# A hybrid encoder layer: block products of the second MLP matrix in turns with quarters of the first, two-tile splits, and a plain last group

## The chip, the cores and the metric

The kernel runs on one core of a Trainium2 chip. The metric is device time in microseconds (us) of one execution. Three executions of the kernel before took 756.33, 757.04 and 757.73 us. A separate execution was profiled; its rows are what is read below. PE is the matrix engine, DVE the vector engine, ACT the scalar engine, POOL the general engine (it also issues transfers that add to their target), SP the queue that issues most plain transfers; PEld is PE's weight load.

## The reference

One encoder layer on 512 tokens of width 1024: a mixer (long convolutions beside dilated attention) and a squared-ReLU MLP, each between RMS norms. The change lies in the MLP and where the mixer hands over to it:

```python
x = x + gt1 * rmsnorm(y, g_post_mix[l])
h = rmsnorm(x, g_pre_mlp[l]) * (1.0 + sc2) + sh2
f = jnp.square(jax.nn.relu(h @ w_mlp1[l])) @ w_mlp2[l]     # 1024 -> 4096 -> 1024
x = x + gt2 * rmsnorm(f, g_post_mlp[l])
```

Everything is float32. PE works on a rounded type (float32r), so each operand is split into a rounded high part and the rest (hi and lo), and a product is three matmuls: hi hi, hi lo, lo hi (`mm3`, L606).

## The kernel before

**How order is set.** The layer is written as a list of operations. `Plan.order` (L291) then chooses, by estimated durations and priorities, one order for each engine, which the engines follow strictly. `plan.bias` and `plan.local` raise priorities; `plan.group` keeps the matmuls of one group at one priority; `_cost` (L529) holds the durations. An operation recorded on `vp` may go to DVE or POOL. Buffers come from named tags with a fixed count (`NB`): `w` 9, `wx` 12, `vx` 12, `cv` 22, `H` 9.

**First MLP product.** `hidden(cc, banks)` (L1383) makes 512 of the 4096 hidden features for all tokens: it loads 8 tiles of `w_mlp1` (256 KB each, on SP, into `raw`), splits each (`whi` by a cast on ACT, `wlo` by a subtraction on DVE or POOL), runs 8 x 4 x 3 = 96 matmuls of 512 columns into four PSUM banks (named `pm`), and squares the relu of the banks into four tiles `r`. There are eight such blocks.

**Second MLP product.** The 4096 features are taken in four groups of two blocks (`sb`). Each group is a product of a 2 x 2 block matrix (token halves by feature blocks) with a 2 x 2 block matrix of weights, done with 7 block products instead of 8. Each block product (`product`, named `pf`) has 4 x 2 x 3 = 24 matmuls into two banks. Some need sums of hidden blocks (`dif`, by `vp`) or of weight blocks. The latter are made by a transfer: `load` puts a weight block into `braw` on SP, and `more` adds another block to it on POOL's queue (`accum_op`). So `braw` of sum "s" serves products 4, 2, 1 and 6, each time after another addition; every user splits it anew into `whi` and `wlo`. The hidden half (128 x 256) is split too (`split_a`, into `ha`, ACT and DVE). Results are added over groups into seven pairs of `acc` tiles (two of them in the buffers of `mask` and `rope`). In the last group each product is added on arrival to the final blocks it belongs to, and a token tile is normalised (`early_half`, `late_half`), gated, added to x and stored once its two halves are there.

**What comes when.** Two blocks of `hidden` are made, then a third, then the 7 products of a group in a row in the order 4, 2, 1, 3, 6, 5, 7, then two more blocks, and so on, with falling priority (`begin`, L1448):

```python
next_hidden()
for sb in range(NS):
    next_hidden()
    next_hidden()
    ...
    product(4, diff(0, A21, A22), load("s", 0, 0))
    product(2, same(A22), more("s", 1, 0))
    product(1, diff(0, A11, D0), more("s", 1, 1))
    ...
```

Of the kernel before, what the change touches and what calls it, by code (L numbers as in the profile page):

```python
# [11 lines left out]
F32 = mybir.dt.float32  # L12
# [210 lines left out]
class Op:  # L223
    __slots__ = ("eng", "call", "dur", "lat", "preds", "succs", "bufs", "new", "n", "rt", "start", "prio", "idx", "move", "urgent", "table", "port", "alt", "group")


class Plan:
# [4 lines left out]
    def __init__(self, nc):  # L232
        self.nc, self.ops, self.tags, self.cnt = nc, [], {}, 0
        self.bias = self.local = 0.0
        self.group = 0
        self.pools = {}
# [17 lines left out]
    def record(self, eng, call, writes, reads, dur, lat=0.0, after=()):  # L254
# [3 lines left out]
        op.port, op.alt, op.group = eng == "gp", None, self.group  # L258
# [32 lines left out]
    def order(self):  # L291
# [58 lines left out]
        while len(done) < len(ops):  # L350
# [44 lines left out]
            if op.move is not None:  # L395

                dma = max(dma, end + 0.65) + op.move
                end = dma + 1.05
# [54 lines left out]
class _Engine:  # L453
# [35 lines left out]
    def __getattr__(self, meth):  # L489
        plan, eng = self.plan, self.eng  # L490

        def rec(*args, after=(), urgent=0.0, **kw):
# [15 lines left out]
            dur, lat = _cost(home, meth, args, kw, writes, reads)  # L508

# [13 lines left out]
            if meth == "dma_start":  # L523
                op.move, op.lat = lat, 0.0
            return op
# [30 lines left out]
def tile_hymba_layer(ctx, tc, t, out):  # L556
# [3 lines left out]
    FILTERS, INPUT, SOON, ROUND, LEAD = 200.0, 1000.0, 9000.0, 3000.0, 30.0  # L560
# [13 lines left out]
    for n in ("basis", "wx"):  # L574
        stage(n, "left")
    for n in ("xp", "hT", "att", "mp"):
        stage(n, "right", side="right")
    NB = {"H": 9, "vx": 12, "qk": 8, "cv": 22, "w": 9, "raw": 4, "ra": 3, "G": 3,
          "x": 8, "xa": 6, "h": 16, "m": 16, "wx": 12}
    HOME = {"x": "xp", "xa": "xp", "h": "hT", "m": "mp", "wx": "wx"}  # L580
# [4 lines left out]
    def R(tag, s="r"):  # L585
        return S(tag, s, F32R)
# [586 lines left out]


# [19 lines left out]
    def group_split(src, gcol, tag):  # L1194
        spl = []
        for i in range(4):
            hi, lo = R(tag, "mh"), R(tag, "ml")
# [35 lines left out]
    NPT = 8  # L1233
# [70 lines left out]
    ma = group_split(att, 108, "cv")  # L1304
# [3 lines left out]
    for tt in range(4):  # L1308
        for hf in range(2):
# [4 lines left out]
    h2T = [(R("m", "h2h"), R("m", "h2l"))  # L1314
           for _ in range(8)]
# [51 lines left out]
    wtags[:] = ["w", "wx"]  # L1367
# [4 lines left out]
    acc, ATAG = {}, ["H"] * 9 + ["G"] + ["cv"] * 2  # L1372
# [10 lines left out]
    def hidden(cc, banks):  # L1383

        ws = [wload(w_1[k * P:(k + 1) * P, cc * 512:cc * 512 + 512]) for k in range(8)]
        for th in range(2) if cc == 0 else (None,):
            ts = slice(0, 512) if th is None else slice(th * 256, th * 256 + 256)
            for k in range(8):
                for i in range(4):
                    s = slice(i * P, (i + 1) * P)  # L1390
                    mm3(banks[i][:, ts], ws[k][0][:, s], ws[k][1][:, s], h2T[k][0][:, ts], h2T[k][1][:, ts], k == 0, k == 7)
        res = []
        for i in range(4):
            r = S("vx", "r")
            act.activation(r, banks[i], AF.Relu)
            vp.tensor_tensor(out=r, in0=r, in1=r, op=ALU.mult)
            res.append(r)
        return res
# [22 lines left out]
    def late_half(tt, a, hf, q, other):  # L1421
# [5 lines left out]
        for i, o in ((1 - hf, other), (hf, g)):  # L1427
# [10 lines left out]
    TO = {1: ((7, 1), (6, 1)), 2: ((2, 1), (6, -1)), 3: ((6, 1), (5, 1)), 4: ((2, 1), (7, 1)), 5: ((7, -1), (5, 1)),  # L1438
          6: ((6, 1),), 7: ((7, 1),)}
    NS, KT = 4, 4  # L1440
    HALF = (slice(0, 256), slice(256, 512))
    NCC = 2 * NS

    hid, piece = {}, [0]

    def begin():  # L1448
        plan.local = LEAD * (NCC + NS - piece[0])
        piece[0] += 1  # L1450
        return piece[0] % 2

    def next_hidden():
        cc = len(hid)
        if cc < NCC:
            hid[cc] = hidden(cc, PS4(begin(), "pm"))
            step(late2)

    next_hidden()
    for sb in range(NS):  # L1460
        next_hidden()
        next_hidden()
        aa, ab = hid[2 * sb], hid[2 * sb + 1]
        last = sb == NS - 1
        tags = ("ps", "pi") if begin() else ("pj", "pj")
        pair = lambda n: [PS("pf", tags[n]) for _ in range(2)]
        wsrc = lambda r, k, c: w_2[sb * 1024 + r * 512 + k * P:sb * 1024 + r * 512 + (k + 1) * P, c * 512:c * 512 + 512]

        pairs = [0]

        def fresh():
            pairs[0] += 1
            plan.group += 1
            return pair((pairs[0] + 1) % 2)

        def add(eng, o, a, b, sign=1):
            eng.tensor_tensor(out=o, in0=a, in1=b, op=ALU.add if sign > 0 else ALU.subtract)

        def product(n, parts, raws):
            banks = fresh()  # L1480
            if last and n == 7:
                ws = [(split_w(raws(k)), parts(k)) for k in range(KT)]
                for i in range(2):
                    for k, ((wh, wl), a) in enumerate(ws):
                        mm3(banks[i], a[:, i * P:(i + 1) * P], a[:, 256 + i * P:256 + (i + 1) * P], wh, wl, k == 0, k == KT - 1)
                    arrive(n, i, banks[i])
                return
            for k in range(KT):
                wh, wl = split_w(raws(k))
                a = parts(k)  # L1490
                for i in range(2):
                    mm3(banks[i], a[:, i * P:(i + 1) * P], a[:, 256 + i * P:256 + (i + 1) * P], wh, wl, k == 0, k == KT - 1)
            for i in range(2):
                arrive(n, i, banks[i])

        def arrive(n, i, bank):
            if not last:
                put(n, i, bank)
                return
            for m, sign in TO[n]:  # L1500
                add(dve, acc[m, i], acc[m, i], bank, sign)

            if n == 2:
# [95 lines left out]
```

## Time and profile before

| what | us |
|---|---|
| median of three runs | 757.04 |
| the profiled execution | 759.21 |
| its span | 757.3 |
| PE busy in the span | 708.6 |
| DVE busy | 573.2 |
| ACT busy | 375.7 |
| POOL busy | 162.6 |
| first block product starts | 452.55 |
| last matmul starts | 746.26 |

The span runs from the first to the last instruction. A busy engine is one that executes; matmuls are pipelined and their ends are modelled, so PE's pace is better read from the number of matmuls that start in a stretch. A wait is idle time of an engine, put down to whatever ended it last. All operations are issued through one helper, line L514, so rows are told apart by the tile names, not by lines.

### The profile page before, as it was taken

To read this page: it belongs to the slowest core of one execution; us is meant where nothing else is said; L and a number is where in the kernel's file an instruction comes from. 1 tells how busy PE (TensorE), PEld (TensorE's weight loads), DVE (VectorE), ACT (ScalarE), POOL (GpSimd) and SP (SyncE) were. 2 spreads that over 40 slices of the span, in tenths; PEclk is the share of its full clock that TensorE was granted. 3 is DMA by queue.
4 is the path that set the end of the run, shared out by engine and by line. 5 is a ranking of instruction groups with operands and counts; after the bars stand their busy time and mean duration, and the time that the engine had idled before them with its cause. 6 is when DMAs were issued, how large, how long until landed. Compare 5 with 4: busy or idle time off the path is not lost. (4 is left out here: it accounts for less than half of the span.)

```text
span 757.3 us, 10569 instructions
## 1 busy us (share of the span) xinstructions
PE 708.6 (94%) x3552; PEld 564.6 (75%) x3552; DVE 573.2 (76%) x1113; ACT 375.7 (50%) x765; POOL 162.6 (21%) x169
## 2 busy tenths in 40 slices
PE   5999999999999999999989998999999999999693
PEld 2667878988897867778879876788777887778472
DVE  5497974989698679997978844656378555898897
ACT  5545442234224478886764524754354434544543
POOL 0120400113032134330120022100242004232440
PEclk9999999999999999999999999999999999999998
DMA  9995244433615363352216547533675337654643
GB/s 287 363 393 183 84 151 155 124 99 115 210 53 167 111 209 99 98 168 71 70 58 199 169 88 147 133 126 126 112 167 128 109 111 132 166 134 92 131 113 124
DMA packets 62518, 109.30 MB, mean 144 GB/s; under 512 B 6621, under 2 KB 15069, under 8 KB 62208
## 3 DMA queue, kind: packets, MB, share of 16 engines
q1 hardware_dynamic: 52096, 87.39, 35.5%
q0 software_dynamic: 10224, 21.18, 15.2%
q8 instruction: 28, 0.46, 0.3%
q14 instruction: 26, 0.21, 0.1%
q10 hardware_dynamic: 144, 0.06, 0.0%
HBM read 104.14 MB, written 4.46 MB: 143 GB/s over the span
## 5 line engine op out<-in xcount | busy, mean ns | idle before, releaser
L514 PE MATMUL pf<-whi,ha 128*128 128x512 f32 x448 | 135.2, 398 | 18.5 <-ACT whi L514 10.5
L514 DVE TENSOR_TENSOR wlo<-braw,whi 128x512 fp32r<-128x512 f32 x112 | 78.8, 725 | 55.4 <-ACT whi L514 49.3
L514 PEld LDWEIGHTS pf<-whi,ha 128*128 128x128 f32 x448 | 83.5, 190 | 44.1 <-ACT whi L514 16.2
L514 ACT CAST whi<-braw 128x512 fp32r<-128x512 f32 x112 | 67.6, 619 | 82.8 <-DMA braw<-in_w_mlp_dram 66.6
L514 ACT CAST whi<-raw 128x512 fp32r<-128x512 f32 x128 | 77.1, 619 | 58.3 <-PE pj L514 27.9
L514 POOL DMA_DIRECT2D braw<-in_w_mlp_dram x64 | 55.9, 929 | 212.5 <-DVE wlo L514 116.4
L514 PE MATMUL pm<-h2h,whi 128*128 128x512 f32 (+1 forms) x288 | 91.8, 374 | 2.9 <-DVE y L514 2.1
L514 DVE TENSOR_TENSOR wlo<-raw,whi 128x512 fp32r<-128x512 f32 x111 | 75.9, 698 | 22.4 <-ACT whi L514 10.7
L514 PE MATMUL pm<-h2l,whi 128*128 128x512 f32 (+1 forms) x288 | 92.1, 374 | 0.0
L514 PE MATMUL pm<-h2h,wlo 128*128 128x512 f32 (+1 forms) x288 | 90.9, 372 | 0.0
L514 PE MATMUL pf<-wlo,ha 128*128 128x512 f32 x224 | 79.0, 396 | 1.6 <-DVE wlo L514 1.6
L514 PEld LDWEIGHTS pm<-h2h,whi 128*128 128x128 f32 x288 | 53.3, 190 | 13.5 <-DVE y L514 2.3
L514 PEld LDWEIGHTS pm<-h2l,whi 128*128 128x128 f32 x288 | 53.4, 190 | 10.8 <-issue 0.5
L514 PEld LDWEIGHTS pm<-h2h,wlo 128*128 128x128 f32 x288 | 53.2, 190 | 10.0
L514 PEld LDWEIGHTS pf<-wlo,ha 128*128 128x128 f32 x224 | 42.2, 189 | 13.5 <-DVE wlo L514 4.9
L514 DVE SCALAR_TENSOR_TENSOR acc<-raw,vec,acc 128x512 f32<-128x512 f32 x56 | 44.5, 795 | 9.1 <-DMA raw<-in_w_ada_dram 8.8
L514 POOL TENSOR_TENSOR wlo<-raw,whi 128x512 fp32r<-128x512 f32 x17 | 23.1, 1365 | 115.6 <-PE pj L514 42.1
L514 DVE TENSOR_TENSOR r<-r 128x512 f32<-128x512 f32 x32 | 21.9, 688 | 29.5 <-ACT r L514 29.4
L514 ACT ACTIVATE r<-pm 128x512 f32<-128x512 f32 x32 | 18.9, 596 | 48.3 <-PE pm L514 48.3
L514 PE MATMUL pj<-hh,whi 128*128 128x512 f32 x96 | 35.2, 397 | 0.9 <-ACT hh L514 0.9
L514 PE MATMUL pj<-hl,whi 128*128 128x512 f32 x96 | 36.0, 400 | 0.0
L514 POOL TENSOR_TENSOR sc<-sc,st 128x512 f32<-128x512 f32 x21 | 24.0, 1160 | 55.5 <-DVE st L514 47.6
(273 smaller groups left out, 1536.9 us busy)
## 6 DMA issues: line engine op xcount, KB each, us to landing
raw<-in_w_ada_dram SPq DMA_DIRECT2D x96, 256.0 KB, 3.5
raw<-in_w_mlp_dram SPq DMA_DIRECT2D x64, 256.0 KB, 3.0
braw<-in_w_mlp_dram POOLq DMA_DIRECT2D x64, 256.0 KB, 4.6
raw<-in_w_in_dram SPq DMA_DIRECT2D x48, 256.0 KB, 3.2
braw<-in_w_mlp_dram SPq DMA_DIRECT2D x48, 256.0 KB, 3.0
raw<-in_w_out_dram SPq DMA_DIRECT2D x16, 256.0 KB, 2.6
H<-hd SPq DMA_DIRECT2D x9, 256.0 KB, 4.9
x<-in_x_dram SPq DMA_DIRECT2D x8, 256.0 KB, 4.6
```

Source lines behind the costliest of these rows:

```text
L514: getattr(e, meth)(*[real(a) for a in args], **{k: real(a) for k, a in kw.items()})
```

## The change

Six things are altered.

1. **Turns.** `hidden` becomes a generator that stops after each quarter (two of its eight weight tiles, 24 matmuls). After two whole blocks, each of the first three groups runs product, quarter, product, quarter, with two quarters after the sixth product. Blocks use the four `pj` banks, products the `ps` and `pi` pairs by turns.
2. **Order of products.** It is 3, 4, 5, 2, 1, 7, 6. The sum "s" is used in turns 2, 4, 5 and 7, the sum "d" in 3 and 6. All differences of hidden blocks are made with product 4.
3. **Two tiles wide.** Hidden features lie in pairs of tiles (`hid`, pool `hp`), and `split_a` and the differences work on 128 x 2 x 256 at once, into `ha` of 8 buffers in pool `mp`.
4. **Last group.** It has no block products: the eight hidden tiles are split whole, both 512-column halves of the output run as plain products (8 x 4 x 3 matmuls each, 192 in all), the sums of the earlier groups (`combine`) are added to four results, and the second half of the depth goes token tile by token tile.
5. **Buffers.** The split of h (`h2T`) moves from pool `mp` to `cv`; the split of the attention output from `cv` to `pt`; weights of the MLP use `w` and `vx` in place of `w` and `wx`, `braw` uses `vx`, and two `acc` tiles move from `cv` to `ra`. The late loads of the last gate (`step(late2)`) come with the first two blocks.
6. **Estimates.** In the MLP 0.09 us is added to each ACT and DVE operation, a summing transfer gets 2.0 us more, and `LEAD`, the step of priority, falls from 30 to 6 for 66 steps. These act on the order only.

How the order on PE changes, in the second group of the MLP (`pf` banks of block products, `pm` of first-product blocks, `ha` and `h2` the hidden and input splits). Before:

```order
L514 MATMUL pf_5808<-wlo_5821,ha_5648 128x512
L514 MATMUL pf_5860<-whi_5817,ha_5521 128x512
L514 MATMUL pf_5808<-whi_5813,ha_5648 128x512
L514 MATMUL pf_5860<-whi_5806,ha_5562 128x512
L514 MATMUL pf_5840<-wlo_5722,ha_5547 128x512
L514 MATMUL pf_5860<-wlo_5833,ha_5562 128x512
L514 MATMUL pf_5840<-whi_5641,ha_5547 128x512
```

Now, at a product of the same group:

```order
L516 MATMUL pm_5556<-h2l_4226,whi_5587 128x512
L516 MATMUL pm_5558<-h2l_4226,whi_5587 128x512
L516 MATMUL pm_5556<-h2h_4204,wlo_5622 128x512
L516 MATMUL pm_5558<-h2h_4204,wlo_5622 128x512
L516 MATMUL pf_5672<-whi_5514,ha_5476 128x512
L516 MATMUL pf_5674<-whi_5514,ha_5476 128x512
L516 MATMUL pf_5672<-wlo_5528,ha_5476 128x512
```

Before, one block product follows on another (three bank sets overlap here); now a quarter of a block stands between two of them.

How the order on POOL changes in the last group (`braw` transfers are summing ones, `acc<-acc,G` the gate). Before:

```order
L514 DMA braw_7061<-in_w_mlp_dram 128x512
L514 DMA braw_7095<-in_w_mlp_dram 128x512
L514 TENSOR_TENSOR ha_7259<-dif_6837,ha_7259 128x256
L514 TENSOR_TENSOR ha_7277<-r_7049,ha_7277 128x256
L514 TENSOR_TENSOR dif_6797<-r_7149,dif_6797 128x256
L514 TENSOR_TENSOR dif_6837<-r_7159,dif_6837 128x256
L514 TENSOR_TENSOR acc_5047<-acc_5047,G_4460 128x512
L514 TENSOR_TENSOR ha_7324<-r_7149,ha_7324 128x256
L514 TENSOR_TENSOR acc_5210<-acc_5210,G_4460 128x512
```

Now:

```order
L516 DMA braw_6235<-in_w_mlp_dram 128x512
L516 TENSOR_TENSOR wlo_6725<-raw_6572,whi_6696 128x512
L516 TENSOR_TENSOR wlo_6796<-raw_6730,whi_6787 128x512
L516 TENSOR_TENSOR acc_5420<-acc_5420,acc_5278 128x512
L516 TENSOR_TENSOR wlo_6922<-raw_6888,whi_6915 128x512
L516 TENSOR_TENSOR wlo_6933<-raw_6869,whi_6908 128x512
L516 TENSOR_TENSOR rope_590<-rope_590,acc_4898 128x512
L516 TENSOR_TENSOR acc_5420<-acc_5420,G_4428 128x512
L516 TENSOR_TENSOR acc_5180<-acc_5180,G_4428 128x512
```

The half-tile work is gone; six operations on whole tiles follow the last summing transfer, and the two gates come last.

The diff, cut to its core:

```diff
-    FILTERS, INPUT, SOON, ROUND, LEAD = 200.0, 1000.0, 9000.0, 3000.0, 30.0
+    FILTERS, INPUT, SOON, ROUND, LEAD = 200.0, 1000.0, 9000.0, 3000.0, 6.0
...
+                op.slow = 2.0 if kw.get("accum_op") is not None else 0.0
...
-    ma = group_split(att, 108, "cv")
+    ma = group_split(att, 108, "pt")
...
-    h2T = [(R("m", "h2h"), R("m", "h2l"))
-           for _ in range(8)]
+    h2T = [(R("cv", "h2h"), R("cv", "h2l")) for _ in range(8)]
...
-    wtags[:] = ["w", "wx"]
+    wtags[:] = ["w", "vx"]
+    plan.fixed = 0.09
...
+    def hidden(cc, banks, res):
+        for kk in range(0, 8, 2) if cc else (0,):
+            if cc == 0:
+                ws = [wload(w_1[k * P:(k + 1) * P, 0:512]) for k in range(8)]
+            else:
+                ws = {k: wload(w_1[k * P:(k + 1) * P, cc * 512:cc * 512 + 512]) for k in (kk, kk + 1)}
...
+            if kk < 6 and cc:
+                yield
...
-        a = R("cv", "ha")
-        act.copy(a[:, 0:256], src)
-        lo_of(vp, a[:, 256:512], src, a[:, 0:256])
+        a = plan.tile("mp", "ha", 8, [P, 2, 2, 256], F32R, "ha")
+        act.copy(a[:, 0], src)
+        lo_of(vp, a[:, 1], src, a[:, 0])
...
+    def begin():
+        moves[0] += 1
+        plan.local = LEAD * (66 - moves[0])
+
+    def block(cc):
+        plan.group += 1
+        gen = hidden(cc, PS4(cc == 0, "pm"), hid[cc])
+        for _ in range(4 if cc else 1):
+            begin()
+            next(gen)
+            yield
...
+        product(3, same(A11), load("b", 0, 1))
+        yield
+        product(4, first, load("s", 0, 0))
+        yield
+        product(5, same(A12), load("d", 1, 1))
+        yield
+        product(2, same(A22), more("s", 1, 0))
+        yield
+        product(1, same(X[2]), more("s", 1, 1))
+        yield
+        product(7, lambda k: split_a(minus(0, A12, X[2], k)), more("d", 1, 0))
+        yield
+        product(6, same(X[1]), more("s", 0, 1))
+        yield
+
+    for sb in range(NS - 1):
+        rest = [s for cc in (2 * sb + 2, 2 * sb + 3) for s in ((block(cc), cc),) * 4]
+        for j, _ in enumerate(products(sb)):
+            for gen, cc in rest[:1 + (j == 5)]:
+                next(gen)
+                rest.pop(0)
+    begin()
+    combine()
...
+    BLOCK = {(0, 0): 7, (0, 1): 5, (1, 0): 2, (1, 1): 6}
+    for hf in range(2):
+        plan.group += 1
+        banks = PS4(1 - hf, "pf")
+        for ks, tts in (((0, 1, 2, 3), ((0, 1, 2, 3),)), ((4, 5, 6, 7), ((0,), (1,), (2,), (3,)))):
+            begin()
...
+                tt = us[0]
+                a = acc[BLOCK[tt // 2, hf], tt % 2]
+                dve.tensor_tensor(out=a, in0=banks[tt], in1=a, op=ALU.add)
+                if hf == 0:
+                    qe[tt] = early_half(tt, a, 0)
+                else:
+                    late_half(tt, a, 1, qe[tt], acc[BLOCK[tt // 2, 0], tt % 2])
```

More of the change, by code (lines that the diff above doesn't have):

```diff
@@ new lines, in tile_hymba_layer, with combine, add @@
+    for cc in range(2):
+        for _ in block(cc):
+            pass
+        step(late2, 1 + cc)
+    qe = {}
+    def combine():
+        for i in range(2):
+            for m in (1, 3, 2):
+                add(vp, acc[6, i], acc[6, i], acc[m, i], -1 if m == 2 else 1)
+            for m in (1, 4, 5):
+                add(vp, acc[7, i], acc[7, i], acc[m, i], -1 if m == 5 else 1)
+            add(vp, acc[2, i], acc[2, i], acc[4, i])
+            add(vp, acc[5, i], acc[5, i], acc[3, i])
+    def add(eng, o, a, b, sign=1):
+        eng.tensor_tensor(out=o, in0=a, in1=b, op=ALU.add if sign > 0 else ALU.subtract)
@@ L1463, in tile_hymba_layer, with products, pair @@
+    turn = [0]
+    def products(sb):
         aa, ab = hid[2 * sb], hid[2 * sb + 1]
-        last = sb == NS - 1
-        tags = ("ps", "pi") if begin() else ("pj", "pj")
-        pair = lambda n: [PS("pf", tags[n]) for _ in range(2)]
+        def pair():
+            turn[0] += 1
+            return [PS("pf", ("ps", "pi")[turn[0] % 2]) for _ in range(2)]
         wsrc = lambda r, k, c: w_2[sb * 1024 + r * 512 + k * P:sb * 1024 + r * 512 + (k + 1) * P, c * 512:c * 512 + 512]
-        pairs = [0]
@@ L1471, in fresh, with product @@
-        def fresh():
-            pairs[0] += 1
+        def product(n, parts, raws):
+            begin()
             plan.group += 1
[L1474 to L1482, printed above, removed]
-                for i in range(2):
[L1484 to L1492, printed above, removed]
-            for i in range(2):
-                arrive(n, i, banks[i])
@@ L1496, in arrive @@
[L1496 to L1503, printed above, removed]
-                qe[2 + i] = early_half(2 + i, acc[2, i], 0)
-            elif n == 6:
-                late_half(2 + i, acc[6, i], 1, qe[2 + i], acc[2, i])
-            elif n == 5:
-                qe[i] = early_half(i, acc[5, i], 1)
-            elif n == 7:
-                late_half(i, acc[7, i], 0, qe[i], acc[5, i])
@@ L1524, in tile_hymba_layer @@
-        X = [S("cv", "dif") for _ in range(KT)]
+            banks = pair()
+            ws = []
+            for k in range(KT):
+                if k % 2 == 0:
+                    a = parts(k // 2)
+                ws.append((a[:, 0, k % 2], a[:, 1, k % 2]) + split_w(raws(k)))
+            for k, (ah, al, wh, wl) in enumerate(ws):
+                for i in range(2):
+                    s = slice(i * P, (i + 1) * P)
+                    mm3(banks[i], ah[:, s], al[:, s], wh, wl, k == 0, k == KT - 1)
@@ L1525, in tile_hymba_layer @@
+            for i in range(2):
+                put(n, i, banks[i])
+        A11, A21 = [[a[:, :, h] for a in aa] for h in HALF]
+        A12, A22 = [[a[:, :, h] for a in ab] for h in HALF]
+        X = [[S("cv", "dif").rearrange("p (a b) -> p a b", a=2) for _ in range(KT // 2)] for _ in range(3)]
         B = {}
@@ L1552, in tile_hymba_layer, with minus, first @@
-        product(3, same(A11), load("b", 0, 1))
-        product(6, diff(1, A21, A11), more("s", 0, 1))
-        product(5, same(A12), load("d", 1, 1))
-        product(7, diff(0, A12, D0), more("d", 1, 0))
-        plan.local = 0.0
+        def minus(o, left, right, k):
+            vp.tensor_tensor(out=X[o][k], in0=left[k], in1=right[k], op=ALU.subtract)
+            return X[o][k]
+        def first(k):
+            a = split_a(minus(0, A21, A22, k))
+            minus(2, A11, X[0], k)
+            minus(1, A21, A11, k)
+            return a
@@ new lines, in products @@
+        yield
+    for sb in range(NS - 1):
[6 more added lines that the diff above has]
+    combine()
+    parts = []
+    for kk in range(8):
+        a = plan.tile("mp", "ha", 8, [P, 2, 512], F32R, "ha")
+        src = hid[2 * NS - 2 + kk // 4][kk % 4 // 2][:, kk % 2]
+        act.copy(a[:, 0], src)
+        lo_of(vp, a[:, 1], src, a[:, 0])
+        parts.append(a)
@@ L1558, in tile_hymba_layer @@
+    plan.local = 0.0
     done = plan.order()
```

96 lines of the change are left out of this document (37 added, 59 removed).

## The prediction

> **What bounds the kernel now.** I read the busy time of each engine by stretch first, with bounds where one stage of the MLP gives way to the next (columns: span, busy time and starts of PE, PEld, DVE, ACT and POOL, granted clock, DMA share, GB/s).
>
> ```profile
> span 757.3 us, 10569 instructions
> ...
> 408.00:452.00 44.00, 44.00 (x191) 35.53 (x189) 30.04 (x63) 19.44 (x40) 4.46 (x6) 1.00 0.53 153
> 452.00:496.00 44.00, 39.88 (x169) 30.66 (x168) 26.15 (x48) 27.20 (x54) 9.53 (x11) 1.00 0.69 147
> 496.00:543.00 47.00, 47.00 (x204) 37.85 (x203) 25.83 (x52) 19.57 (x41) 5.21 (x6) 1.00 0.39 112
> 543.00:588.00 45.00, 41.01 (x173) 31.23 (x172) 32.93 (x57) 21.62 (x45) 14.02 (x16) 1.00 0.68 149
> 588.00:634.00 46.00, 46.00 (x199) 36.88 (x198) 25.37 (x49) 18.22 (x36) 6.67 (x8) 1.00 0.41 109
> 634.00:676.00 42.00, 38.19 (x163) 29.73 (x162) 33.96 (x61) 21.78 (x45) 13.90 (x15) 1.00 0.69 155
> 696.00:716.80 20.80, 14.27 (x60) 10.65 (x58) 17.90 (x30) 10.45 (x24) 10.93 (x13) 0.99 0.82 150
> 716.80:746.60 29.80, 28.11 (x112) 21.68 (x112) 27.72 (x46) 14.52 (x33) 10.13 (x10) 0.95 0.38 90
> 746.60:757.30 10.70, 0.04 (x1) 0.00 (x0) 6.72 (x13) 1.52 (x6) 0.00 (x0) 0.69 0.46 172
> ```
>
> In the first-product stretches (408, 496, 588) PE is never idle and starts a 512-wide matmul every 47/204 = 0.2305 us. In the block-product stretches (452, 543, 634) and the last group (696 to 746.6) it starts fewer. Time lost there, span minus starts times 0.2305: 5.05, 5.12 and 4.43 us, together 14.6, and 50.6 - 172 x 0.2305 = 10.9 us in the last group. So PE bounds the MLP, and 25.5 us of it is spent unfed. Next, what PE waited for from 452 us on (total, times, longest), and the largest wait of ACT:
>
> ```profile
> PE pf L514 <- ACT whi L514: 10.5, 9, 2.0
> PE pf L514 <- DVE acc L514: 5.9, 4, 4.2
> PE pf L514 <- ACT ha L514: 1.8, 1, 1.8
> PE pf L514 <- DVE wlo L514: 1.6, 3, 0.8
> ...
> ACT whi L514 <- DMA braw<-in_w_mlp_dram: 61.6, 47, 5.7
> ```
>
> Mostly PE waits for split weights of a block product, and ACT, which makes their high part, waits for the summing transfer into braw. The costs per instruction (mean ns behind the busy time) and the time from issue to landing, of the summing transfers on POOL and of a plain load on SP:
>
> ```profile
> L514 DVE TENSOR_TENSOR wlo<-braw,whi 128x512 fp32r<-128x512 f32 x112 | 78.8, 725 | 55.4 <-ACT whi L514 49.3 <-PE pm L514 5.3 <-ACT ha L514 0.6
> L514 ACT CAST whi<-braw 128x512 fp32r<-128x512 f32 x112 | 67.6, 619 | 82.8 <-DMA braw<-in_w_mlp_dram 66.6 <-PE pm L514 8.8 <-PE pf L514 3.1
> L514 DVE TENSOR_TENSOR wlo<-raw,whi 128x512 fp32r<-128x512 f32 x54 | 37.0, 699 | 10.5 <-ACT whi L514 4.5 <-ACT r L514 1.8 <-ACT ha L514 1.2
> L514 DVE TENSOR_TENSOR ha<-dif,ha 128x256 fp32r<-128x256 f32 x58 | 25.0, 448 | 1.6 <-ACT ha L514 1.2
> L514 DVE TENSOR_TENSOR ha<-r,ha 128x256 fp32r<-128x256 f32 x39 | 20.4, 538 | 2.2 <-ACT ha L514 2.0
> L514 DVE TENSOR_TENSOR acc<-pf,acc 128x512 f32<-128x512 f32 x24 | 16.1, 683 | 1.2 <-PE pf L514 1.1
> L514 DVE TENSOR_TENSOR dif<-r,dif 128x256 f32<-128x256 f32 x30 | 12.2, 421 | 0.3
> L514 DVE TENSOR_TENSOR r<-r 128x512 f32<-128x512 f32 x32 | 21.9, 688 | 29.5 <-ACT r L514 29.4
> L514 POOL TENSOR_TENSOR wlo<-raw,whi 128x512 fp32r<-128x512 f32 x5 | 7.3, 1468 | 22.8 <-ACT whi L514 21.3 <-DVE wlo L514 1.5
> ...
> DMA to landing us min/median/max: 2.5/4.3/9.2
> ...
> raw<-in_w_mlp_dram SPq DMA_DIRECT2D x64, 256.0 KB, 3.0
> ```
>
> **Part one: the turns.** A block product is 24 matmuls, 5.53 us. Its DVE work before: 4 weight splits 2.90, 4 splits of hidden halves at about 0.49 = 1.96, 2 sums 1.37, and 16/7 differences 0.96: 7.2 us, 130% of PE's time, less what POOL takes. It lives on work done ahead in the stretch before. After, a turn is a product and a quarter block, 48 matmuls, 11.06 us. DVE: 2.90 + 2 two-tile splits at 0.70 (not in the trace; bounds are one and two halves, 0.45 and 1.08, I take the 512-wide row) 1.40 + sums 1.37 + 8/7 wide differences 0.80 + 2 weight splits 1.40 + one square 0.69 = 8.6 us, 77%. ACT: 6 weight casts, 2 casts of two tiles and one relu at about 0.62 each, 5.6 us, 51%. Neither bounds.
>
> The chain of one summed weight is landing 4.3 + cast 0.62 + split 0.73 + about 0.2 between engines = 5.9 us, or 10.8 at the longest landing. Before, products 4, 2, 1 use the same sum one after another, 5.5 us apart: even the median does not fit. The new order 3, 4, 5, 2, 1, 7, 6 leaves two turns (22 us) before 2, 7, three before 6, and one (11.06 us) only between 2 and 1. So of the 14.6 us I keep one mean ACT wait, 10.5/9 = 1.2 us, at that place in each of three groups: 3.6. Bounds: 0 (10.8 fits in 11.06) and half of the old loss, 7.3.
>
> **Part two: the last group.** It goes from 168 to 192 matmuls: 24 x 0.2305 = +5.5 us, wholly on PE. In return its 16 summing transfers on POOL's queue become 4 more plain loads on SP, 28 weight splits become 16, and 24 sums from PSUM become 8. Where its 10.9 us went:
>
> ```profile
> 710.40 4.63 DVE L514 TENSOR_TENSOR ha<-r,ha 128x256 fp32r<-128x256 f32 x1
> ...
> 710.40 1.07 POOL L514 TENSOR_TENSOR ha<-dif,ha 128x256 fp32r<-128x256 f32 x1
> 711.10 1.06 POOL L514 TENSOR_TENSOR ha<-r,ha 128x256 fp32r<-128x256 f32 x1
> 711.79 1.73 POOL L514 TENSOR_TENSOR dif<-r,dif 128x256 f32<-128x256 f32 x2
> 713.17 1.56 POOL L514 TENSOR_TENSOR acc<-acc,G 128x512 f32<-128x512 f32 x1
> ...
> 716.87 1.22 PE L514 MATMUL pf<-whi,ha 128*128 128x512 f32 x2 [4.18 <-DVE acc L514]
> 717.89 0.63 PE L514 MATMUL pf<-wlo,ha 128*128 128x512 f32 x1
> 718.32 1.05 PE L514 MATMUL pf<-whi,ha 128*128 128x512 f32 x2
> ```
>
> One half-tile split on DVE took 4.63 us instead of 0.54, while five POOL operations ran back to back; the sums behind it came late, no bank was free, and PE stood 4.18 us and then started matmuls 0.43 us apart (717.89 to 718.32) at a lower granted clock. The half-tile operations of that run no longer exist in the last group, and all four banks of a half stand free. I take the 10.9 us as regained, and charge the three wlo waits, 1.6 us, for the plain group's weights and 1.2 us for the last hidden block's split, which now stands right before its use; bounds 0 and 5.4. What is late next is the DVE sums of the earlier groups into the four results; 48 matmuls (11 us) of the first weights cover 16 of them at 0.68.
>
> **Part three: the end.**
>
> ```profile
> 746.26 0.39 PE L514 MATMUL pf<-whi,ha 128*128 128x512 f32 x1
> ...
> 747.83 0.68 DVE L514 TENSOR_TENSOR rope<-rope,pf 128x512 f32<-128x512 f32 x1
> ...
> 748.55 0.63 ACT L514 ACTIVATE junk<-rope 128x512 bf16<-128x512 f32 x1 [1.42 <-DVE rope L514]
> ...
> 752.60 0.75 DVE L514 SCALAR_TENSOR_TENSOR g<-g,sf,xr 128x512 f32<-128x512 f32 x1
> 753.38 0.33 SPq L514 DMA_DIRECT2D out_dram<-g  x1
> ```
>
> From the last matmul's start to the last issue it is 7.1 us, since the sum queues behind other tiles' work (747.83) and the final steps of several tiles follow. After, tiles finish one at a time: 0.39 for the matmul and about 0.2 to DVE, some 0.65 each (the 0.68 and 0.75 of the rows overlap their neighbours by 0.1) for sum, product and four final steps, 0.1 for a reciprocal and 0.1 to the issue: 4.7 us. Gain 2.4 (bounds 0 and 3.5).
>
> **Part four: up to the first block.** The split of h moves to other buffers, the first blocks' weights share theirs with y.
>
> ```profile
> 382.43 0.58 PE L514 MATMUL pm<-h2h,whi 128*128 128x256 f32 x1 [2.10 <-DVE y L514]
> ```
>
> PE waits here for a bank that holds y. In the new order that matmul's bank comes ten rows of 256-wide matmuls later, about 1.2 us. I take 1.0 us gained; bounds 3.8 (the wait and the half-clock starts after it) and -2 (the same wait once more, for buffers). The rest of the change I cost at nothing: weight buffers are 21 in both, and PE is fed without a gap there (408 to 452); without that cover a pair that comes late costs a load, cast and split, 3.0 + 0.62 + 0.70 = 4.3 us once. The loads of w_mlp2 now stand between those of w_mlp1 on SP, 4 more in all; they wait there for free buffers only, and their 3.0 us is well inside a turn.
>
> **Sum.** 5.5 - 14.6 + 3.6 - 10.9 + 2.8 - 2.4 - 1.0 = -17.0 us. The profiled execution took 759.21, 1.9 over its span of 757.3; the runs' median, 757.04, lies next to the span. So I predict 757.04 - 17.0 = **740.0 us** (profiled: about 742, span about 740).
>
> **Rivals.** *Supply stays late* (16%): half the old loss remains, 7.3 + 5.4 instead of 6.4 us: 746.3. For it: landings in bursts reached 9.2 us. Against: the one-turn spacing holds even that.
>
> *POOL blocks DVE again* (12%): the new POOL order ends in a row of six two-tile operations. Should they run unbroken, at 1.468 us each, DVE stands 8.8 us instead of the 1.2 charged: 747.6. Against: their inputs become ready ten ACT casts apart. The Trainium skill, page "SBUF — State Buffer", section "Who interferes with whom", says that a DVE instruction with two SBUF inputs and a GpSimd one that reads SBUF block each other for a whole instruction. The 4.63 us row goes further: DVE stood through five in a row.
>
> *Smooth* (9%): no waits remain, and the bank wait at 382 goes too: about 733.
>
> *Slower* (6%): now hidden quarters queue on in-order DVE and ACT behind block weights. One late landing then stops the squares and the sums that free banks, where before the first-product stretches ran with no loss. It decides from 17.0/12 = 1.4 us at each of the 12 dependent products of three groups; at 2.5 us each, 770. Against: DVE has 23% free.
>
> *Clock* (2%): bank pairs change some 42 times. If each change idled PE into the half clock, 8 matmuls at 0.43 instead of 0.23 cost 1.6 us each, 67 us: 807. Against: granted clock 1.00 in all three block stretches with their 5 us of waits. The Trainium skill, page "TensorE: Matmul & The Clock Gate", section "A second HAM failure mode: psum-queue depth-cycling", describes such a loss from cycling banks; the trace has bank changes without it.
>
> *No effect* (3%): the order does alternate, but what is regained only pays for the 24 matmuls: 757.
>
> **How the numbers follow.** The forecast has 52%, its own range 735 to 745. Faster: 52 + 16 + 12 + 9 = 89%. Within 0.2% (1.5 us, what a measurement of this kernel tells from none): 3%. Slower: 8%. Range 732 to 750: the forecast, both partial cases and most of the smooth one.
>
> **What would show it.** In the new profile: stretches of block products with 0.2305 us per matmul and under 2 us of waits per group; the last group 44 to 48 us long; no DVE row above 2 us there; under 9 us from the last matmul to the end. Wrong if PE waits for whi or sums remain above 13 us, or the stretch before 408 us grows.

## The result, and the profile after

The changed kernel took **732.96 us** (four runs, 732.56 to 733.22) where the kernel before took 757.38 beside it (756.33 to 760.85): ratio **0.9669, 95% interval 0.9638 to 0.9701**. The forecast was 740.0 in 732 to 750. The profiled execution took 732.56 us with a span of 730.8; before, 759.21 and 757.3.

By stretch (columns as in the prediction: span, busy time and starts of PE, PEld, DVE, ACT and POOL, granted clock, DMA share, GB/s), bounds at the first product, two places inside the turns, the last turn, the last first-product matmul and the last matmul:

```profile
408.00:427.80 19.80, 19.80 (x89) 16.41 (x88) 15.91 (x26) 7.74 (x14) 0.91 (x1) 1.00 0.61 204
427.80:500.00 72.20, 72.20 (x313) 58.70 (x313) 40.01 (x61) 36.52 (x66) 14.34 (x16) 1.00 0.59 140
500.00:573.00 73.00, 73.00 (x318) 59.72 (x317) 48.05 (x73) 35.85 (x63) 19.08 (x20) 1.00 0.63 144
573.00:637.00 64.00, 64.00 (x278) 52.16 (x277) 42.49 (x65) 30.18 (x53) 18.39 (x20) 1.00 0.63 147
637.00:678.00 41.00, 41.00 (x179) 33.26 (x178) 31.64 (x44) 19.98 (x35) 10.55 (x9) 1.00 0.38 111
678.00:722.30 44.30, 44.30 (x192) 35.66 (x190) 24.34 (x42) 10.91 (x26) 2.60 (x2) 1.00 0.15 54
722.30:730.80 8.50, 0.10 (x1) 0.00 (x0) 4.57 (x9) 1.75 (x6) 0.00 (x0) 0.67 0.33 124
```

PE is busy in every microsecond from 408 to 722.3 and starts a matmul every 72.20/313 = 0.2307 us, at full clock; the last group (678 to 722.3) starts 192 in 44.3 us, where before it started 172 in 50.6. What PE waited for between 370 and 735 us:

```profile
PE ph L516 <- DVE dg L516: 0.7, 1, 0.7
PE pm L516 <- DVE y L516: 0.5, 1, 0.5
PE pm L516 <- POOL h2l L516: 0.3, 1, 0.3
PE pm L516 <- ACT h2h L516: 0.2, 1, 0.2
```

All four lie ahead of the MLP's wide matmuls. No wait for `whi`, `wlo`, `ha` or `acc` is left. The groups that answer to those of before, among them the two-tile split that the prediction had to estimate (711 ns against the 0.70 us taken):

```profile
L516 DVE TENSOR_TENSOR wlo<-braw,whi 128x512 fp32r<-128x512 f32 x79 | 57.1, 726 | 47.6 <-ACT whi L516 34.2 <-issue 6.5 <-PE pm L516 3.5
L516 ACT CAST whi<-braw 128x512 fp32r<-128x512 f32 x84 | 50.9, 621 | 62.5 <-DMA braw<-in_w_mlp_dram 29.7 <-PE pm L516 17.3 <-DVE wlo L516 7.0
L516 DVE TENSOR_TENSOR ha<-dif,ha 128x512 fp32r<-128x512 f32 x23 | 16.3, 711 | 3.9 <-ACT ha L516 3.9
```

ACT's wait for the transfers into `braw` fell from 66.6 to 29.7 us. Both kinds of transfer are in these figures, and the trace tells them apart by the queue that issued the one a cast waited for: before, 42.6 us were for summing transfers and 24.1 for plain loads; now all 29.7 are for plain loads and none for summing ones. The summing transfers did not get quicker. From issue to landing (the last figure, the median), before and now:

```profile
braw<-in_w_mlp_dram POOLq DMA_DIRECT2D x64, 256.0 KB, 4.6
braw<-in_w_mlp_dram POOLq DMA_DIRECT2D x48, 256.0 KB, 4.7
```

The two ends of the MLP, its first 512-wide matmul and the tail behind the last one:

```profile
405.83 0.63 PE L516 MATMUL pm<-h2h,whi 128*128 128x512 f32 x2
...
722.01 0.39 PE L516 MATMUL pf<-whi,ha 128*128 128x512 f32 x1
...
722.63 0.68 DVE L516 TENSOR_TENSOR rope<-pf,rope 128x512 f32<-128x512 f32 x1
723.34 0.63 ACT L516 ACTIVATE junk<-rope 128x512 bf16<-128x512 f32 x1 [0.28 <-DVE rope L516]
...
726.27 0.74 DVE L516 SCALAR_TENSOR_TENSOR g<-g,sf,xr 128x512 f32<-128x512 f32 x1
...
727.04 0.33 SPq L516 DMA_DIRECT2D out_dram<-g  x1
```

The span shrank by 757.3 - 730.8 = 26.5 us. To compare kernels I take the last 1368 matmuls into `pm` and `pf` (1344 where the last group has block products), from the start of the first to the start of the last, and call this the *MLP piece*. In the changed kernel it begins with the first 512-wide matmul. It begins 1.6 us earlier than before (405.83 against 407.43), takes 316.2 us in place of 338.8, 22.6 less although it holds 24 more matmuls, and from the last matmul to the end it is 8.8 in place of 11.1 us.

### The profile page after: what moved, and what is told of

The parts are those of the page before. It is cut to its first block, busy times and chain, and to the rows that moved or that the text cites. A ratio compares the mean times of both kernels' runs of the same rounds, so it can differ in the third digit from the quotient of the medians.

```text
span 730.8 us, 10377 instructions
## 1 busy us (share of the span) xinstructions
PE 705.9 (97%) x3576; PEld 570.2 (78%) x3576; DVE 536.4 (73%) x987; ACT 357.9 (49%) x691; POOL 149.5 (20%) x149
## 4 chain that ended last, share of the span: by engine, by line
PE 85%; DVE 6%; DMA 4%; ACT 3%; issue 1%; SPq 1%; POOL 0%; DVEq 0%; ACTq 0%; POOLq 0%
PE pm L516 23%; PE pf L516 22%; PE pj L516 17%; PE pw L516 6%; PE pH L516 4%; PE inv L516 2%; PE pav L516 2%; PE s L474 2%; DMA raw<-in_w_in_dram 2%; PE pe L516 2%; DMA raw<-in_w_ada_dram 2%; PE ptr L462 2%; PE po L516 1%; DMA x<-in_x_dram 1%; PE pa L516 1%
## 5 line engine op out<-in xcount | busy, mean ns | idle before, releaser
L516 PE MATMUL pf<-whi,ha 128*128 128x512 f32 x464 | 143.2, 395 | 0.0
L516 ACT CAST whi<-raw 128x512 fp32r<-128x512 f32 x144 | 87.8, 621 | 76.4 <-PE pj L516 28.2
L516 DVE TENSOR_TENSOR wlo<-raw,whi 128x512 fp32r<-128x512 f32 x124 | 85.8, 704 | 35.1 <-ACT whi L516 15.8
L516 PEld LDWEIGHTS pf<-whi,ha 128*128 128x128 f32 x464 | 87.4, 188 | 20.4 <-issue 0.2
L516 DVE TENSOR_TENSOR wlo<-braw,whi 128x512 fp32r<-128x512 f32 x79 | 57.1, 726 | 47.6 <-ACT whi L516 34.2
L516 ACT CAST whi<-braw 128x512 fp32r<-128x512 f32 x84 | 50.9, 621 | 62.5 <-DMA braw<-in_w_mlp_dram 29.7
L516 POOL DMA_DIRECT2D braw<-in_w_mlp_dram x48 | 41.9, 908 | 152.8 <-DVE wlo L516 131.4
L516 POOL TENSOR_TENSOR wlo<-raw,whi 128x512 fp32r<-128x512 f32 x20 | 27.0, 1352 | 136.8 <-ACT whi L516 61.2
L516 DVE SCALAR_TENSOR_TENSOR acc<-raw,vec,acc 128x512 f32<-128x512 f32 x56 | 43.9, 783 | 8.5 <-DMA raw<-in_w_ada_dram 8.2
L516 PE MATMUL pj<-whi,hh 128*128 128x512 f32 x96 | 35.1, 400 | 0.4 <-DVE y L516 0.4
L516 PE MATMUL pj<-hh,wlo 128*128 128x512 f32 x96 | 35.4, 397 | 0.0
```

The source lines that it names most:

```text
L516: getattr(e, meth)(*[real(a) for a in args], **{k: real(a) for k, a in kw.items()})
```

## The experiments

The experiments ran in three groups, each on a chip of its own. These chips ran the kernel before in 762 to 764 us (medians 761.95, 762.12 and 763.64), some 5 us more than above; the changed kernel, run again in the third group, took 733.24, as above. So kernels are compared by their ratio to the kernel before beside them and by the MLP piece of their profiles; a difference of two medians from different groups is the weaker measure.

| kernel | us | ratio to before, interval | MLP piece |
|---|---|---|---|
| before (beside the result) | 757.38 | 1 | 338.8 (24 matmuls fewer) |
| changed, once more | 733.24 | 0.9606 (0.9572-0.9640) | 316.7 |
| turns, old order of products | 734.10 | 0.9637 (0.9615-0.9660) | 316.1 |
| no turns, new order | 739.23 | 0.9708 (0.9677-0.9739) | 322.7 |
| no turns, old order | 733.08 | 0.9628 (0.9602-0.9654) | 315.5 |
| the same, one tile wide | 733.74 | 0.9624 (0.9564-0.9684) | 317.4 |
| turns, old costs | 737.43 | 0.9656 (0.9615-0.9697) | 319.9 |
| no turns, old order, old costs | 754.61 | 0.9885 (0.9850-0.9921) | 338.5 |
| before, new summing cost | 741.80 | 0.9718 (0.9681-0.9754) | 324.7 (24 fewer) |
| before, both new costs | 743.32 | 0.9743 (0.9690-0.9796) | 321.2 (24 fewer) |
| block products in the last group | 740.42 | 0.9725 (0.9700-0.9751) | 322.2 (24 fewer) |
| changed, old costs and step 30 | 756.74 | 0.9919 (0.9897-0.9942) | 321.2 |
| no turns, old costs and step 30 | 767.92 | 1.0076 (1.0050-1.0101) | 333.8 |

### Turns and the order of products

The theory was the prediction's: PE outran the supply of split weights, and turns double the time for it. The rival was that the new sequence of products did the work. Three kernels take the two apart. Without turns, blocks and products follow as before (three blocks, seven products, two blocks, ...):

```diff
-        for j, _ in enumerate(products(sb)):
-            for gen, cc in rest[:1 + (j == 5)]:
-                next(gen)
-                rest.pop(0)
+        for _ in products(sb):
+            pass
...
+        for gen, cc in rest:
+            next(gen)
```

> The changed kernel without its turns: three blocks of the first product first, then the seven products of a group in a row (order kept: 3, 4, 5, 2, 1, 7, 6), two blocks, and so on, as the kernel before had it. All else stays. Theory 'turns' (PE outran the supply of split weights, and a turn doubles the time for it): waits of PE for whi, wlo and sums come back. DVE has 2.90 + 1.40 + 1.37 + 0.80 = 6.5 us of work per product against 7.2 before, for 5.53 us of matmuls; of before's 14.6 us this is 14.6 x 1.0/1.7 = 8.5, so 741.5 us (737 to 748). Theory 'order' (the new sequence of products and the two-tile operations were enough): no more than 3 us lost, 733 to 736.

It took 739.23 us, inside the first theory's range, with waits back on PE from 452 us on:

```profile
PE pf L516 <- ACT whi L516: 2.7, 2, 2.3
PE pf L516 <- DVE wlo L516: 1.1, 1, 1.1
PE pf L516 <- DVE acc L516: 0.3, 1, 0.3
```

Read alone this is support. The next two kernels are the same without and with turns, with the old sequence:

```diff
-        product(3, same(A11), load("b", 0, 1))
...
         product(4, first, load("s", 0, 0))
...
         product(2, same(A22), more("s", 1, 0))
...
         product(1, same(X[2]), more("s", 1, 1))
...
+        product(3, same(A11), load("b", 0, 1))
+        product(6, same(X[1]), more("s", 0, 1))
+        product(5, same(A12), load("d", 1, 1))
+        product(7, lambda k: split_a(minus(0, A12, X[2], k)), more("d", 1, 0))
```

> The changed kernel without turns and with the old order of products, 4, 2, 1, 3, 6, 5, 7. Sum 's' is then used three times 5.5 us apart. Theory 'turns': as without turns alone plus one wait or two of 1 to 2 us per group for a late summing transfer, 745 us (740 to 752), with PE's waits for whi above those of the row in new order. Theory 'order': this is the kernel that brings most of the loss back, 747, and it alone; the row in new order is near 733.

> The changed kernel with its turns, but the old order of products, 4, 2, 1, 3, 6, 5, 7. The sums are then one turn, 11.06 us, apart at 4-2, 2-1 and 5-7; the chain of a summed weight is 5.9 us at the median landing and 8.6 at 7.0 us, the longest of the changed kernel. Theory 'turns': it fits, 733 to 735. Theory 'order': the wait returns at three places per group, 1.2 us or more each, 9 x 1.2 = 11, so 744.

In a row and in the old order, as the kernel before had it, it took 733.08 us, as fast as the changed kernel, and its trace shows PE no wait at all from 452 us on. The theories had said 745 and 747. With turns the old order took 734.10, as the first theory said. So neither turns nor their order are needed for the gain; the new order costs 6 us when products stand in a row (739.23 against 733.08) and nothing in turns. Why it costs 6 in a row was not followed up; its summing transfers landed after 6.1 us in the median, against 4.9 in the old order.

"In a row" is the order of the program, and the planner does not keep all of it: in the kernels without turns and in the old order, with new costs and with old ones, it mixes the sixth product with matmuls of the first product and puts some 40 to 70 of them before the seventh. The products 4, 2 and 1 do stand in a row. In the first group of the old order they start at 450.5, 456.3 and 461.9 us, and the first weight of the second and the third is split by 448.6 and 457.1: made ahead.

### The last group

```diff
-    for hf in range(2):
-        banks = PS4(1 - hf, "pf")
...
+    for _ in products(NS - 1):
+        pass
...
+            for m, sign in TO[n]:
+                add(dve, acc[m, i], acc[m, i], bank, sign)
```

> The changed kernel with the last group as seven block products in a row again (order 3, 4, 5, 2, 1, 7, 6, two-tile splits, each product added on arrival to the results it belongs to, the last product bank by bank), 24 matmuls fewer. Turns in the first three groups stay. Theory of the prediction: the plain group regained 10.9 + 2.4 us for 5.5 + about 0.3, so +7.5 us, 740.5 (737 to 744), with waits of PE for sums or whi after the last block and over 10 us from the last matmul to the end. Rival: with two-tile operations and the new order the block products of the last group would have been fed as well; then the 24 matmuls are saved for nothing, 733 - 5.5 + 2 = 729.5.

It took 740.42 us: 7.2 more than the changed kernel on another chip (about 9 by the two ratios), against 7.5 expected; the rival's 729.5 is out. From the last matmul to the end it is 9.4 us, where over 10 were expected. Its last group, and PE's waits from 452 us on:

```profile
678.60:729.20 50.60, 42.21 (x168) 31.72 (x166) 46.47 (x72) 23.89 (x48) 31.52 (x28) 0.96 0.64 126
```

```profile
PE pf L516 <- DVE wlo L516: 5.5, 2, 2.8
PE pf L516 <- ACT whi L516: 2.7, 2, 1.8
PE pf L516 <- DVE ha L516: 0.2, 1, 0.2
```

168 matmuls take 50.6 us, as long as before (50.6 there too), and DVE is busy 46.47 of them, 92%. The size was right. The cause I had read in the profile before, a DVE operation held up by a run of POOL ones and sums that came late, is not the one here: PE waits for `wlo` and `whi`, not for sums. The group looks short of DVE time, where the plain group needs 24.34 us of it in 44.3. But this is argued, not shown: DVE's 15 weight splits take 920 ns in the mean here, the longest 2.16 us with two POOL operations beside it, against 726 in the changed kernel's MLP, and no run separates too much work on DVE from DVE held up beside POOL.

### What feeds the row

If not turns, something else in the kernel without turns had removed some 20 us. Two parts were left that work there: operations two tiles wide (less DVE work), and the estimates, by which the planner sets its order. Beside them stand the buffers. The estimates undone, and the widths undone, each from the kernel without turns in old order:

```diff
-    plan.fixed = 0.09
+    plan.fixed = 0.0
...
-                op.slow = 2.0 if kw.get("accum_op") is not None else 0.0
+                op.slow = 0.0 if kw.get("accum_op") is not None else 0.0
...
-    FILTERS, INPUT, SOON, ROUND, LEAD = 200.0, 1000.0, 9000.0, 3000.0, 6.0
+    FILTERS, INPUT, SOON, ROUND, LEAD = 200.0, 1000.0, 9000.0, 3000.0, 30.0
```

> The kernel without turns and with the old order of products (which ran as fast as the changed kernel, 733.1 us) with the planner's old estimates: nothing added to ACT and DVE operations, nothing to a summing transfer, step of priority 30. The orders on the engines change, no work does. Theory 'estimates' (before, ACT stood 62.9 us in its order at transfers into braw that landed later than planned; with the new estimates 22.2 us): the waits come back, some 5 us in each of three groups, 745 us (740 to 748), ACT's wait for braw above 45 us. Theory 'two tiles wide' or 'buffers': nothing comes back, 733 to 735.

```diff
-        act.copy(a[:, 0], src)
-        lo_of(vp, a[:, 1], src, a[:, 0])
+        for k in range(2):
+            act.copy(a[:, 0, k], src[:, k])
+            lo_of(vp, a[:, 1, k], src[:, k], a[:, 0, k])
```

> The same kernel (no turns, old order of products, new estimates) with the splits of hidden halves and the differences one tile wide again: 4 splits and 16/7 differences per product at 0.49 and 0.42 us in place of 2 and 8/7 at 0.70. Theory 'two tiles wide' (DVE's 7.2 us of work per product of 5.5 us was the limit, 6.5 is still over it but the work done ahead now suffices): waits come back, 5 us in a group or more, 745 us. Theory 'estimates': no change beyond 2 us, 733 to 735.

One tile wide it took 733.74 us, with one wait of 0.9 us for `whi`: the 7.2 us of DVE work per 5.53 us product, which I had called 130%, do not starve PE. With the old estimates it took 767.92. The estimates then went into the kernel before (two of three), and out of the changed one:

```diff
-                end = dma + 1.05
+                end = dma + 1.05 + op.slow
...
+            if home in ("act", "dve"):
+                dur += plan.fixed
...
+                op.slow = 2.0 if kw.get("accum_op") is not None else 0.0
...
+    plan.fixed = 0.09
```

> The kernel before with two of the three new estimates alone: 0.09 us more for each ACT and DVE operation of the MLP and 2.0 us more for a summing transfer; the step of priority stays at 30. No operation, buffer or size changes. Theory 'estimates': 8 to 14 us less than before, ratio 0.982 to 0.989, PE's waits for whi in the three block-product stretches under 4 us. Theory 'two tiles wide' or 'buffers': ratio 0.997 to 1.003.

> The changed kernel, turns and new order of products included, with the planner's old estimates and step 30. If the turns give slack enough that late landings do no harm: 733 to 736 us. If the estimates carry the gain with turns as well: 740 to 748, with waits of PE for whi or wlo at the products of sum 's'.

Two numbers that no engine ever sees took 18.8 us off the kernel before (743.32 against 762.12, ratio 0.9743), more than the 8 to 14 expected, and PE's waits for `whi` in the block-product stretches fell to 0.9 us. And the changed kernel without its estimates is at 756.74, almost all the gain gone, against 740 to 748 at the most. This last was a poor experiment: 65 steps of 30 put the start of the MLP 1950 ahead of everything else, where 12 of 30 (360) stood before and 65 of 6 (390) stand now. Its trace shows the price ahead of the MLP, between 370 and 452 us:

```profile
PE pm L516 <- DVE h L516: 3.6, 1, 3.6
PE pm L516 <- ACT h2h L516: 3.2, 3, 1.3
PE pm L516 <- DVE y L516: 1.9, 1, 1.9
```

PE starts 512-wide matmuls at 407.15 us there and at 408.30 in the kernel without turns, then goes back to the mixer and to 256-wide ones, and comes to the 26th 512-wide matmul only at 425.7 and 427.0, where the changed kernel has it at 411.5: 14.2 and 15.5 us late. (The 17 us of an expectation below, "ahead of the first 512-wide matmul", is the start of the MLP piece, 422.7 and 424.0 us, which in these two kernels lies among 256-wide matmuls.) What the costs did can't be read from these two runs.

### Costs alone, with and without turns

So the costs were undone once more with the step at 6, with turns and without, beside the changed kernel itself, and of the two costs the summing transfer's 2.0 us was put alone into the kernel before.

> The changed kernel once more, beside the runs of this group: 733 us (732 to 735), and from the first 512-wide matmul of the MLP to the last matmul 316 us, as in its first profile. It is here to be compared with the three others on the same chip.

```diff
-    plan.fixed = 0.09
+    plan.fixed = 0.0
...
-                op.slow = 2.0 if kw.get("accum_op") is not None else 0.0
+                op.slow = 0.0 if kw.get("accum_op") is not None else 0.0
```

> The changed kernel, turns included, with the old costs in the plan: nothing added to ACT and DVE operations, nothing to a summing transfer. The step of priority stays at 6 (with 66 steps it spans about what 30 with 12 steps spanned before, so 30 was no fair undoing: it cost 17 us ahead of the first 512-wide matmul). Theory 'either cure': turns give a late landing 11 us of room, so the plan's error does little harm, 733 to 738 us, the stretch from the first 512-wide matmul to the last matmul at most 321. Theory 'costs alone': the waits come back with turns too, 743 to 750. Theory 'step': 733, and the run without turns as well.

> The kernel without turns and with the old order of products, with the old costs in the plan as above, step 6. Theory 'either cure' and theory 'costs alone': without turns nothing makes up for transfers that land later than planned; of the 18 us that the stretch grew with old costs and step 30, 10 to 18 come back, 743 to 751 us, with PE's waits for whi and wlo above 6 us. Theory 'step': the loss was the step's, 733 to 736.

```diff
-                end = dma + 1.05
+                end = dma + 1.05 + op.slow
...
+                op.slow = 2.0 if kw.get("accum_op") is not None else 0.0
```

> The kernel before with one new cost alone: 2.0 us more for a summing transfer. With 0.09 us per ACT and DVE operation beside it the ratio was 0.974. If the summing transfer's cost carries that gain, as ACT's waits for braw (62.9 us before, 35.4 with both costs) say: ratio 0.970 to 0.983. If the 0.09 us carries it (some 600 operations of DVE in the MLP, 54 us of work that the plan did not count): 0.99 to 1.0.

Four medians, of which 733.08 is from the first group of runs and the others from the third:

| us | old costs | new costs |
|---|---|---|
| products in a row, old order | 754.61 | 733.08 |
| turns, new order | 737.43 | 733.24 |

*Either cure* is right, within its ranges but for the row, 3.6 us past its upper end. With old costs the turns (with the new order) take 17.2 us off; with new costs they take nothing off. The costs take 21.5 off without turns (20 by the ratios 0.9885 and 0.9628) and 4.2 with them. Most of those 4.2 is no wait for a block product's weights: PE's one long wait in turns with old costs is at 441.7 us, for a sum of the last gate, and from 432 to 452 us it starts 76 matmuls, against 86 in the changed kernel run beside it (10 x 0.231 = 2.3 us):

```profile
PE pa L516 <- DVE acc L516: 1.8, 1, 1.8
```

And 2.0 us in one line takes the kernel before from 763.64 to 741.80: the summing transfer's cost carries all that both costs gave (0.9718 against 0.9743). The 0.09 us was not run alone. Against turns with old costs at step 6, step 30 made the changed kernel with old costs 19 us slower (756.74 against 737.43, on two chips).

What the cost does is seen on ACT. The plan counts 1.04 us for a summing transfer's issue, 0.65 ahead of it, 256 KB at 0.73 us and 1.05 behind it (the queue free, L397 and L398, `_cost`): 3.5 us from the start of the issue, with the 2.0 us 5.5. The traces of all runs say 4.6 to 5.2 in the median for summing transfers (6.1 in the row in new order) and up to 9.3. ACT runs its list strictly in order, so a cast that stands where the plan believes its data to be there stops everything behind it. The cast's group in the row with old costs, in the row with new ones, and in turns with old ones:

```profile
L516 ACT CAST whi<-braw 128x512 fp32r<-128x512 f32 x84 | 50.2, 619 | 78.0 <-DMA braw<-in_w_mlp_dram 66.4 <-PE pm L516 6.3 <-PE pf L516 1.9
```

```profile
L516 ACT CAST whi<-braw 128x512 fp32r<-128x512 f32 x84 | 50.1, 620 | 39.5 <-DMA braw<-in_w_mlp_dram 22.2 <-PE pm L516 9.6 <-DVE wlo L516 3.0
```

```profile
L516 ACT CAST whi<-braw 128x512 fp32r<-128x512 f32 x84 | 51.0, 620 | 77.7 <-DMA braw<-in_w_mlp_dram 43.9 <-PE pm L516 22.8 <-PE pf L516 5.7
```

The same 84 casts of the same length wait 66.4 us for the transfers in the first, as the 112 of the kernel before did (66.6), and 22.2 in the second. Of these, 51.7 and 8.8 us are for summing transfers, the rest for plain loads. In the kernel before, the 2.0 us alone brought ACT's wait for summing transfers from 42.6 to 13.9 us. The median landing of the summing ones is 5.1 us in the row with old costs and 4.9 with new: not the transfers changed, but where their casts stand. In the third ACT still waits 43.9 us, but 42.5 of them are for plain loads: with a quarter block between two products the summing transfers have nearly always landed when their casts come up. From 452 us on PE waits for a block product's operand once, 0.3 us. In the row with old costs, first ACT alone, then the rows of PE (bracket: idle before, and what ended it):

```profile
461.88 0.62 ACT L516 CAST ha<-hid 128x512 fp32r<-128x512 f32 x1 [0.31 <-PE pf L516]
467.11 1.14 ACT L516 CAST whi<-braw 128x512 fp32r<-128x512 f32 x2 [4.61 <-DMA braw<-in_w_mlp_dram]
468.15 1.06 ACT L516 COPY acc<-pf 128x512 f32<-128x512 f32 x2
...
473.62 1.66 ACT L516 CAST whi<-braw 128x512 fp32r<-128x512 f32 x3 [2.32 <-DMA braw<-in_w_mlp_dram]
```

```profile
475.33 1.22 PE L516 MATMUL pf<-whi,ha 128*128 128x512 f32 x2 [2.50 <-ACT whi L516]
476.35 0.63 PE L516 MATMUL pf<-wlo,ha 128*128 128x512 f32 x1
476.77 1.05 PE L516 MATMUL pf<-whi,ha 128*128 128x512 f32 x2
```

ACT stands 4.61 us, the copies of finished sums (468.15) wait behind it, it stands again for 2.32, and PE waits 2.50. Then PE goes on at half pace, 476.77 - 476.35 = 0.42 us a matmul. PE's waits from 452 us on, and the three stretches of block products, show that this counts:

```profile
PE pf L516 <- ACT whi L516: 6.9, 5, 2.6
PE pf L516 <- DVE wlo L516: 2.0, 1, 2.0
PE pm L516 <- ACT whi L516: 1.0, 2, 0.6
PE pm L516 <- DVE wlo L516: 0.3, 1, 0.3
```

```profile
452.00:488.00 36.00, 33.34 (x133) 25.24 (x131) 20.74 (x33) 20.94 (x39) 10.25 (x12) 0.95 0.76 146
543.00:579.00 36.00, 32.91 (x124) 24.59 (x123) 22.81 (x37) 14.74 (x27) 11.58 (x13) 0.91 0.71 142
641.00:684.00 43.00, 38.83 (x149) 29.20 (x148) 32.94 (x53) 19.04 (x34) 9.55 (x9) 0.92 0.56 134
```

115 us less 406 starts times 0.2305 is 21.4 us lost, and the waits listed are 10.2: about half of the price of these waits is paid after them, at a lower granted clock (0.91 to 0.95). The clock stands at half for 3.4, 6.8 and 6.9 us behind the waits of 2.50, 2.63 and 1.97 us, which costs 8.5 us; the second of these spells:

```profile
564.10:570.90 6.80, 6.48 (x15) 4.68 (x16) 3.77 (x7) 3.58 (x7) 1.10 (x1) 0.50 0.25 86
```

DVE is busy for 58%, 63% and 77% of the three stretches, so over each of them it had time to spare.

## Why the prediction was right, and where it was not

The direction and the range held, and the profile did what the section on what would show it asked for: 0.2307 us a matmul in the turns, no waits, a last group of 44.3 us without a DVE row above 2 us, 8.8 us from the last matmul's start to the end. The time came out where the rival *smooth* had it (about 733, given 9%), below the forecast's own 735 to 745 and 1 us inside the range. Point by point:

**The turns: right size, wrong limit, and one cure too many.** That PE waits for weights whose summing transfer holds up ACT was read rightly, and the turns cure it: with the old costs they take 17.2 us off, and ACT's wait for summing transfers falls from 51.7 us to 1.4. The step that failed is "Before, products 4, 2, 1 use the same sum one after another, 5.5 us apart: even the median does not fit", with the 130% of DVE beside it. (The 4.3 us in that step takes plain loads in; the summing transfers alone have 4.6 in the median, so the chain is 6.2 us, longer still.) Both are arguments on rates, and the row in old order refutes them at once: same sum, 5.6 and 5.8 us apart, no wait, and one tile wide none over 0.9 us. Weights were made ahead; what broke the row was that ACT stood in its fixed order behind transfers that the plan expected 1.1 to 1.7 us too early in the median. Item 6 of the change, the estimates, removes that as well, and I had left it in "the rest of the change I cost at nothing" without a row for it. Beside the turns it is worth 4.2 us, most of them at the wait for the last gate.

**The waits kept: 3.6 and 2.8 us, measured 0.** I kept a mean ACT wait in each group because landings come in bursts, and a wait and a half in the last group. With two cures in one kernel nothing was left to wait. This is 6.4 of the 9.5 us by which the span shrank more than forecast (26.5 against 17.0).

**The loss before: 25.5 us, measured 28.2.** Of the rest, most is the measure of it. I took the starts in windows times 0.2305, and a window also counts matmuls that straddle its bounds, up to three in each; and 1.3 us were lost in the stretches that I had taken as full. From start to start, the changed kernel's MLP piece has 1369 steps in 316.2 us (two matmuls of the last gate among them), 0.2310 each; the 1345 steps before took 338.8 us and at this pace would have taken 310.6, so 28.2 us were lost, 2.7 more than I had. Less 24 x 0.2310 = 5.5 us for the added matmuls, which the forecast had to the tenth, that is the 22.6 us by which the piece shrank.

**The last group: right in sum, not in cause.** Its terms gave 5.5 - 10.9 + 2.8 - 2.4 = -5.0 us, without the waits kept -7.8; the run that undoes it says 7.2, on another chip. The stall under five POOL operations was real in that execution, but a last group of block products takes as long without it.

**The two ends.** From the last matmul to the end 2.3 us were gained (2.4 forecast), and 1.6 up to the start of the MLP piece (1.0). The 0.6 us beyond the forecast is no more than this point varies by: 405.8 in the first profile of the changed kernel, 406.4 in the second.

**The rivals.** *Slower* feared that late landings stop ACT and DVE with the quarters' work behind them. ACT was stopped for 29.7 us, all before casts of plain loads, and no wait of PE followed. *POOL blocks DVE again*: the longest DVE row of the last group is 1.75 us. *Supply stays late*: no wait for weights is left. *Clock*: the granted clock is 1.00 from 408 to 722.3 us, through all 40 and more changes of bank.

**What stays open.** The kernel before took 762 to 764 us on the three chips of the experiments and 757 beside the result, the changed kernel 733 in both places; which of its waits grew was not profiled. No version was found that beats the changed kernel by more than the intervals: the row with new costs and old order has 0.9628 (0.9602 to 0.9654) against 0.9606 (0.9572 to 0.9640).

## What to carry to other kernels

Where a planner fixes the order of in-order engines, its estimates are part of the kernel: compare each planned latency with its median landing in the trace, each kind of transfer by itself, before reading an engine's wait as a lack of speed. A ratio of work over 100% in a stretch starves nobody as long as work done ahead covers it; look at that engine's busy share in the stretch, and at what ended its idle time. And a kernel with two cures needs both undone, one by one and together, since each alone looks as if it did nothing or everything.

## What the runs showed that I had not expected

A wait of PE can cost twice its length: behind the 2.50 us wait above matmuls start 0.42 us apart, and in the row with old costs 10.2 us of waits go with 21.4 us of loss. It need not: in the kernel before, 19.8 us of waits from 452 us on go with 28.2 us of loss, and the waits of up to 2.0 us in its block-product stretches left the granted clock at 1.00.

A DVE operation stood through a run of POOL operations once more, in the kernel before with the new summing cost:

```profile
701.16 1.40 POOL L516 TENSOR_TENSOR ha<-r,ha 128x256 fp32r<-128x256 f32 x1
701.42 3.46 DVE L516 TENSOR_TENSOR ha<-r,ha 128x256 fp32r<-128x256 f32 x1
...
702.14 2.44 POOL L516 TENSOR_TENSOR ha<-dif,ha 128x256 fp32r<-128x256 f32 x3
...
705.53 0.50 PE L516 MATMUL pf<-wlo,ha 128*128 128x512 f32 x1 [2.69 <-DVE wlo L516]
```

A half-tile split of 0.54 us in the mean took 3.46 while four POOL operations with two inputs ran one after another, the split of the next weight came late, and PE waited 2.69 us. That makes two such places (4.63 us under five before). The Trainium skill, page "SBUF — State Buffer", section "Who interferes with whom", has the two engines block each other for one instruction; the two rows here are longer than one. No kernel that keeps POOL out of that stretch was run, so the cause is read from the rows and not shown.
